# Start addresses of the matmul operands of a two-layer encoder, and the form of its weight list

## The chip, the core and the metric

The kernel runs on one core of one Trainium2 chip. The metric is the time of one execution on the device in microseconds; three executions of the kernel before are given below. The names of the engines are those of the profile: PE is TensorE (its matmuls; PEld are its weight loads), DVE is VectorE, ACT is ScalarE, POOL is GpSimd and SP is SyncE, whose queue SPq issues most transfers.

## The reference, cut to what matters

Two layers over 256 tokens of width 2048. Each layer is a token mixer and a gated MLP with a width-3 convolution over tokens; each is preceded by an RMS norm and added to the residual.

```python
for i in range(DEPTH):                       # DEPTH = 2, D = 2048, F = 5632
    h = rmsnorm(x, mix_norm_g[i])
    if i % 2 == 0:
        x = x + short_conv_mixer(h, ...)     # h @ (D, 3D), gates and conv, @ (D, D)
    else:
        x = x + dilated_attention_mixer(h, ...)  # h @ (D, 9D), 16 heads x 3 groups, @ (D, D)
    h = rmsnorm(x, ffn_norm_g[i])
    u = dwconv3(h @ w_up[i], ...)            # (D, 2F)
    a, b = split(u, 2)
    x = x + (silu(a) * b) @ w_down[i]        # (F, D)
return rmsnorm(x, final_norm_g)
```

Nearly all the arithmetic is in the products with the weight matrices, and each weight is read from device memory once and used once, for all 256 tokens.

## The kernel before

Activations are held transposed: a tile has 128 features on the partitions and the 256 tokens along the row. To keep more than the precision of the type float32r (four bytes an element), both operands of a product are split in a rounded part *hi* and a rest *lo*, so that a value is hi + lo. An activation row for one block k of 128 features holds 256 hi values and behind them 256 lo values, 512 in all (2048 bytes). Such tiles are `h` (input of the projections), `y` (input of the short convolution's output projection), `a` (input of the MLP's down projection, two buffers) and `o` (the attention's output). In `mm` these rows are the moving operand of TensorE, and a block of 128 x 128 weights is the stationary one, which PEld loads.

`load_w` fetches one column block of a weight matrix (1 MB, or 704 KB for the down projection) in a tile `raw` (four buffers) over the SP queue. `split` then makes, for up to 8 blocks at a time, the hi weights on ACT (line 72, a copy with rounding) and the lo weights on DVE (line 73, `raw - hi`), both into one tile `w2` (tag `w2`, four buffers): 8 hi blocks of 512 bytes, and behind them 8 lo blocks.

`mm` works through the tiles `w2` one after the other. For the blocks `now` that lie in the present tile it issues first the *hi matmuls*, each 512 columns wide (hi weights times the hi and lo halves of the row, line 102), then the *lo matmuls*, 256 columns wide (lo weights times the hi half, line 104). All add up in one tile `ps` in PSUM; `gathered` adds its two halves. The list that tells which blocks lie together is `parts`, pairs of a tile and a number, and the test is

```python
now = [k for k in ks if parts[k][0] is w2]
```

One hi matmul and its lo matmul are called a *pair* below. There are 5072 pairs with `h`, 1232 with `a`, 256 with `y` and 256 with `o`. Besides these:

- The first block of columns of the short convolution (lines 89 and 90, tile `w2s`) has 48 pairs in which hi and lo matmuls alternate, since there weights arrive block by block.
- The values of the attention (`v_unit`, lines 365 and 368, tile `w2v`, same buffers as `w2`) have the roles exchanged: `h` is stationary, the weights move. 768 pairs.
- The last quarter of the second layer's down projection (`last`, lines 242 to 244) issues, for each block, three matmuls of 256 columns in the order hi, lo, hi: 528 matmuls.

Pools are laid out in the row of a partition in the order in which they and their tiles are asked for: `const` (with `x`, `h` and small tiles), `weights` (`raw`, `w2`), `temps`, and behind them the pool of the running layer part (`y`, `a`, `o`, ...). Where the tiles begin follows from the sizes of all before them. The tile framework sets semaphores; each engine runs its instructions in the order of the program.

Of the kernel before, what the change touches and what calls it, by code (L numbers as in the profile page):

```python
# [10 lines left out]
F32 = mybir.dt.float32  # L11
F32R = mybir.dt.float32r
# [4 lines left out]
P = 128  # L17
T = 256
D = 2048
KT = D // P  # L20
FF = 5632
NF = FF // P
CH = 11
# [4 lines left out]
ALIBI_MAX = 8.0  # L28
SLOPES = [float(v) for v in (2.0 ** (-ALIBI_MAX * np.arange(1, H + 1) / H)).astype(np.float32)]
RAW = 4  # L30
QSCALE = float(P) ** -0.5


@with_exitstack
def encoder_kernel(ctx: ExitStack, tc: tile.TileContext, xT, gs, scw, fcw, dist, w_first, w_in, w_so, w_v, w_qk, w_ao, w_up, w_dn, out):
# [3 lines left out]
    pe, dve, act = nc.tensor, nc.vector, nc.scalar  # L39

    cp = ctx.enter_context(tc.tile_pool(name="const", bufs=1))
    wp = ctx.enter_context(tc.tile_pool(name="weights", bufs=1))
    tp = ctx.enter_context(tc.tile_pool(name="temps", bufs=2))
    pp = ctx.enter_context(tc.tile_pool(name="psum", bufs=4, space=bass.MemoryType.PSUM))

    x = cp.tile([P, KT, T], F32, name="x")
    h = cp.tile([P, KT, 2 * T], F32R, name="h")
    g_sb = cp.tile([P, 5, KT], F32, name="g_sb")
    scw_sb = cp.tile([P, KT, 4], F32, name="scw_sb")
    fcw_sb = cp.tile([P, 2, 2 * NF, 4], F32, name="fcw_sb")  # L50
    ones = cp.tile([P, P], F32, name="ones")
    ident = cp.tile([P, P], F32, name="ident")
    acc = cp.tile([P, T], F32, name="acc")
    rr = cp.tile([P, T], F32, name="rr")
    eps = cp.tile([P, 2], F32, name="eps")
    rc = cp.tile([P, 2], F32, name="rc")

    dve.memset(ones, 1.0)
    dve.memset(eps, EPS)
# [8 lines left out]
    def f32(ap):  # L68
        return ap.bitcast(F32)

    def split(hi, lo, src):
        ins = act.copy(hi, src)  # L72
        dve.tensor_sub(lo, src, f32(hi))  # L73
        return ins


    def load_w(src, n):
        raw = wp.tile([P, KT, P], F32, name="raw", tag="raw", bufs=RAW)
        nc.sync.dma_start(raw[:, :n, :], src)
        parts = []  # L80
        for k0 in range(0, n, 8):
            m = min(8, n - k0)
            w2 = wp.tile([P, 2, 8, P], F32R, name="w2", tag="w2", bufs=4)
            split(w2[:, 0, :m, :], w2[:, 1, :m, :], raw[:, k0 : k0 + m, :])
            parts += [(w2, k) for k in range(m)]
        return parts

    def mm1(ps, w, a, start, stop):
# [3 lines left out]
    def mm(ps, parts, a, ks):  # L92


        n = len(parts)
        ks = list(ks)
        while ks:
            w2 = parts[ks[0]][0]
            now = [k for k in ks if parts[k][0] is w2]
            ks = ks[len(now) :]  # L100
            for k in now:
                pe.matmul(ps, w2[:, 0, parts[k][1], :], a[:, k, :], start=k == 0, stop=False)  # L102
            for k in now:
                ins = pe.matmul(ps[:, :T], w2[:, 1, parts[k][1], :], a[:, k, :T], start=False, stop=k == n - 1)  # L104
        return ins

    def new_ps():
        return pp.tile([P, 2 * T], F32, name="ps", tag="ps", bufs=4)
# [31 lines left out]
    def squares(j):  # L140
        if j == 0:
            act.square(acc, x[:, j, :])
        else:
            sq = tp.tile([P, T], F32, name="sq", tag="sq")
            act.square(sq, x[:, j, :])
            dve.tensor_add(acc, acc, sq)
# [5 lines left out]
    def newton(r, v, t, whole=True):  # L152

        dve.tensor_mul(t, r, r)
        dve.tensor_mul(t, t, v)
        dve.tensor_scalar(t, t, -0.5, 1.5, op0=ALU.mult, op1=ALU.add)
        if whole:
            dve.tensor_mul(r, r, t)
# [78 lines left out]
    def last(ps, parts, a, j):  # L237

        xj = x[:, j, :]
        for k in range(CH):  # L240
            w2, i = parts[k]
            pe.matmul(ps[:, :T], w2[:, 0, i, :], a[:, k, T:], start=k == 0, stop=False)  # L242
            pe.matmul(ps[:, :T], w2[:, 1, i, :], a[:, k, :T], start=False, stop=False)  # L243
            pe.matmul(ps[:, :T], w2[:, 0, i, :], a[:, k, :T], start=False, stop=k == CH - 1)  # L244
        dve.tensor_add(xj, xj, ps[:, :T])
        if j < KT - 1:
            squares(j)
            act.mul(xj, xj, g_sb[:, 4, j : j + 1])
            return
        sq = tp.tile([P, T], F32, name="sq", tag="sq")  # L250
        act.square(sq, xj)
        st = pp.tile([P, 2 * T], F32, name="stat", tag="s", bufs=2)
        for n, src in enumerate((acc, sq)):
            for i in range(2):
                pe.matmul(
                    st[:, i : i + 1], src[:, i * P : (i + 1) * P], ones[:, 0:1], start=n == 0 and i == 0, stop=n == 1 and i == 1
                )
        dve.tensor_scalar_mul(xj, xj, g_sb[:, 4, j : j + 1])
        v = tp.tile([P, 2], F32, name="v", tag="m")
        dve.tensor_scalar(v, st[:, :2], 1.0 / D, EPS, op0=ALU.mult, op1=ALU.add)  # L260
        act.activation(rc, st[:, :2], AF.Sqrt, bias=eps[:, 0:1], scale=1.0 / D)
        dve.reciprocal(rc, rc)
        t = tp.tile([P, 2], F32, name="t", tag="den")
        newton(rc, v, t, False)

        dg = tp.tile([P, T], F32, name="dg", tag="e0")
        for i in range(2):
            dve.tensor_scalar(
                dg[:, i * P : (i + 1) * P], ident, rc[:, i : i + 1], t[:, i : i + 1], op0=ALU.mult, op1=ALU.mult
            )  # L270
        rb = pp.tile([P, 2 * T], F32, name="rb", tag="s", bufs=2)
        pe.matmul(rb[:, :T], ones, dg, start=True, stop=True)
        k0 = 0
        for n in (1, 2, 3, 4, 4, 2):
            ks = slice(k0, k0 + n)
            dve.tensor_mul(x[:, ks, :], x[:, ks, :], rb[:, :T].rearrange("p (a t) -> p a t", a=1).broadcast_to((P, n, T)))  # L276
            nc.sync.dma_start(out[:, ks, :], x[:, ks, :])
            k0 += n
# [50 lines left out]
    def attention():  # L329
        with tc.tile_pool(name="att", bufs=1) as sp:  # L330
# [9 lines left out]
            def norms():  # L340
                rms()
                dve.tensor_copy(rp.rearrange("p (i m) -> p i m", i=2), rr.rearrange("p (m i) -> p i m", i=2))
                dve.tensor_scalar_mul(rq, rp, QSCALE)
                for i in range(2):
                    ps = pp.tile([P, 2 * T], F32, name="stat", tag="s", bufs=2)
                    pe.transpose(ps[:, :P], rp[:, i * P : (i + 1) * P], ident)
                    dve.tensor_copy(rc[:, i : i + 1], ps[:, 0:1])

            def v_unit(hp, g):

                first = hp == 0 and g == 0
                if g == 0:
                    v = sp.tile([P, 2, 2, T], F32R, name="v", tag="v0", bufs=2)
                else:
                    v = sp.tile([P, 2, T], F32, name="v", tag=f"v{g}", bufs=2)
                ps = [new_ps(), new_ps()]
                for k0 in range(0, KT, 8):
                    raw = wp.tile([P, 8, T], F32, name="rawv", tag="raw", bufs=RAW)
                    nc.sync.dma_start(raw, w_v[3 * hp + g, :, k0 * T : (k0 + 8) * T])
                    for k1 in range(k0, k0 + 8, 4):  # L360
                        w2 = wp.tile([P, 4, 2, T], F32R, name="w2v", tag="w2", bufs=4)
                        split(w2[:, :, 0, :], w2[:, :, 1, :], raw[:, k1 - k0 : k1 - k0 + 4, :])
                        for k in range(k1, k1 + 4):
                            for i in range(2):
                                pe.matmul(ps[i], h[:, k, i * P : (i + 1) * P], w2[:, k - k1, :, :], start=k == 0, stop=False)  # L365
                        for k in range(k1, k1 + 4):
                            for i in range(2):
                                pe.matmul(  # L368
                                    ps[i][:, :T], h[:, k, T + i * P : T + (i + 1) * P], w2[:, k - k1, 0, :],
                                    start=False, stop=k == KT - 1,  # L370
                                )
                if first:
                    norms()
                for i in range(2):
                    tmp = tp.tile([P, T], F32, name="tmp", tag="tmp")
                    act.mul(tmp, ps[i][:, T:], rc[:, i : i + 1])
                    e = tp.tile([P, T], F32, name="e", tag="e0") if g == 0 else v[:, i, :]
                    dve.scalar_tensor_tensor(e, ps[i][:, :T], rc[:, i : i + 1], tmp, op0=ALU.mult, op1=ALU.add)
                    if g == 0:
                        split(v[:, i, 0, :], v[:, i, 1, :], e)  # L380
                vs[hp, g] = v
# [101 lines left out]
            for j in range(2):  # L483
                w = load_w(w_ao[j], KT)
                ps = new_ps()
# [5 lines left out]
            for j in range(KT):  # L491
                if j < 2:
                    ps, w = first[j]
                    mm(ps, w, o, range(KT - 1, KT))
                else:
                    w = load_w(w_ao[j], KT)
                    ps = new_ps()
# [90 lines left out]
```

## Time and profile before

| | |
|---|---|
| median of 3 executions | 2828.83 us (2828.40 to 2829.21) |
| the profiled execution | 2828.65 us, of which 2826.9 us from first to last instruction (span) |
| mean granted TensorE clock | 0.998 |
| PE busy / weight loads | 2810.6 us (99%) / 2465.7 us, 16388 each |
| DVE busy | 1995.9 us (71%) |
| ACT busy | 1505.3 us (53%) |
| bytes moved | 519.5 MB, 184 GB/s |

The page gives the time of a matmul from its start to a modelled end, and matmuls are pipelined: the next starts before the end of the last (a 512-column matmul is given 396 ns, but eight of them in a row start within less than 2 us). What a matmul costs is therefore read from start to start: in the timeline, where equal instructions that follow each other stand in one row with their first start, the difference of the starts of two rows divided by the count is the cost of one.

### The profile page before, as it was taken

What the parts mean: (1) busy time and instruction counts of PE and PEld (TensorE: products, weight loads), DVE (VectorE), ACT (ScalarE), POOL (GpSimd) and SP (SyncE); (2) the same over time, 40 slices, a digit from 0 to 9 for tenths busy, and PEclk for the clock granted to TensorE, in tenths of its full rate; (3) what the DMA queues carried; (4) which work ended last, traced back from release to release, by engine and by line L of the source; (5) the groups of instructions that cost most, each with busy time, mean ns of one, the idle gap of its engine ahead of it and who ended that gap; (6) DMA issues with size and microseconds to landing.
All of it is one profiled execution on the core that took longest, in us unless ns stands there. A gap on an engine that the chain in (4) does not pass through costs nothing.

```text
span 2826.9 us, 40841 instructions
## 1 busy us (share of the span) xinstructions
PE 2810.6 (99%) x16388; PEld 2465.7 (87%) x16388; DVE 1995.9 (71%) x3065; ACT 1505.3 (53%) x2320; POOL 0.7 (0%) x6
## 2 busy tenths in 40 slices
PE   9999999999999999999999999999999999999998
PEld 7888888888888888888888888888888888888888
DVE  7676787876867768665665666666778876777865
ACT  6444565555555546544444444444565555555555
POOL 0000000000000000000000000000000000000000
PEclk9999999999999999999999999999999999999999
DMA  7555555546555456544454454454455546546454
GB/s 254 199 181 192 191 183 192 182 166 214 184 166 210 168 186 218 182 175 170 174 178 168 175 179 167 176 179 168 175 190 184 193 161 211 188 164 214 169 181 143
DMA packets 79822, 519.50 MB, mean 184 GB/s; under 512 B 9104, under 2 KB 10256, under 8 KB 28816
## 3 DMA queue, kind: packets, MB, share of 16 engines
q1 hardware_dynamic: 79488, 516.37, 52.0%
q8 instruction: 128, 2.10, 0.3%
q14 instruction: 62, 0.51, 0.1%
q10 hardware_dynamic: 144, 0.52, 0.0%
HBM read 514.76 MB, written 2.10 MB: 183 GB/s over the span
## 4 chain that ended last, share of the span: by engine, by line
PE 99%; DMA 1%; DVE 0%; ACT 0%; SPq 0%; issue 0%; DVEq 0%; ACTq 0%
PE ps L102 56%; PE ps L104 28%; PE ps L365 6%; PE ps L368 3%; PE ps L242 1%; PE ps L244 1%; PE ps L243 1%; PE ot L456 1%; PE s L414 1%; PE pt L433 0%; PE ot L451 0%; DMA raw<-in_w_first 0%; DMA raw<-in_w_in 0%; DVE x L276 0%; PE s L400 0%; PE s L402 0%
## 5 line engine op out<-in xcount | busy, mean ns | idle before, releaser
L73 DVE TENSOR_TENSOR w<-raw,w 128x1024 fp32r<-128x1024 f32 (+1 forms) x954 | 1082.1, 1134 | 391.4 <-ACT w L72 372.5
L102 PE MATMUL ps<-h,w 128*128 128x512 f32 x5072 | 1289.6, 396 | 0.1
L72 ACT CAST w<-raw 128x1024 fp32r<-128x1024 f32 (+1 forms) x954 | 934.9, 980 | 553.5 <-PE ps L104 434.6
L102 PEld LDWEIGHTS ps<-h,w 128*128 128x128 f32 x5072 | 909.7, 188 | 169.0 <-ACT w L72 0.4
L104 PEld LDWEIGHTS ps<-h,w 128*128 128x128 f32 x5072 | 689.8, 188 | 58.2
L104 PE MATMUL ps<-h,w 128*128 128x256 f32 x5072 | 704.1, 281 | 0.0
L112 ACT COPY tmp<-ps 128x256 f32<-128x256 f32 x464 | 172.4, 372 | 500.4 <-PE ps L104 500.1
L114 DVE TENSOR_TENSOR e<-ps,tmp 128x256 f32<-128x256 f32 x464 | 196.2, 423 | 253.2 <-ACT tmp L112 253.2
L102 PE MATMUL ps<-a,w 128*128 128x512 f32 x1232 | 322.6, 394 | 0.0
L102 PEld LDWEIGHTS ps<-a,w 128*128 128x128 f32 x1232 | 215.4, 188 | 34.2
L365 PE MATMUL ps<-w2v,h 128*128 128x512 f32 x768 | 195.5, 396 | 0.0
L104 PEld LDWEIGHTS ps<-a,w 128*128 128x128 f32 x1232 | 175.8, 188 | 20.4
L73 DVE TENSOR_TENSOR w2v<-rawv,w2v 128x1024 fp32r<-128x1024 f32 x96 | 117.6, 1225 | 99.9 <-ACT w2v L72 98.5
L104 PE MATMUL ps<-a,w 128*128 128x256 f32 x1232 | 179.8, 279 | 0.0
L365 PEld LDWEIGHTS ps<-w2v,h 128*128 128x128 f32 x768 | 137.8, 188 | 25.3
L72 ACT CAST w2v<-rawv 128x1024 fp32r<-128x1024 f32 x96 | 100.7, 1049 | 97.6 <-PE ps L368 70.5
L368 PEld LDWEIGHTS ps<-w2v,h 128*128 128x128 f32 x768 | 104.6, 188 | 8.9
L126 ACT ACTIVATE cv<-e,fcw_sb 128x256 f32<-128x256 f32 x176 | 105.8, 602 | 12.1 <-DVE e L121 11.9
L368 PE MATMUL ps<-w2v,h 128*128 128x256 f32 x768 | 106.9, 281 | 0.0
L121 DVE TENSOR_TENSOR e<-e,rr 128x256 f32<-128x256 f32 x220 | 93.0, 424 | 6.8
L127 DVE SCALAR_TENSOR_TENSOR cv<-e,fcw_sb,cv 128x255 f32<-128x255 f32 x176 | 84.1, 479 | 8.0 <-ACT cv L126 8.0
L128 DVE SCALAR_TENSOR_TENSOR cv<-e,fcw_sb,cv 128x255 f32<-128x255 f32 x176 | 85.0, 484 | 6.1
(120 smaller groups left out, 1553.1 us busy)
## 6 DMA issues: line engine op xcount, KB each, us to landing
raw<-in_w_up SPq DMA_DIRECT2D x176, 1024.0 KB, 4.8
raw<-in_w_qk SPq DMA_DIRECT2D x96, 1024.0 KB, 4.8
raw<-in_w_dn SPq DMA_DIRECT2D x128, 704.0 KB, 4.0
rawv<-in_w_v SPq DMA_DIRECT2D x48, 1024.0 KB, 5.0
raw<-in_w_in SPq DMA_DIRECT2D x45, 1024.0 KB, 4.8
raw<-in_w_so SPq DMA_DIRECT2D x16, 1024.0 KB, 4.8
raw<-in_w_ao SPq DMA_DIRECT2D x16, 1024.0 KB, 4.7
raw<-in_w_first SPq DMA_DIRECT2D x3, 384.0 KB, 5.3
```

What stands on the lines that cost most here:

```text
L72: ins = act.copy(hi, src)
L73: dve.tensor_sub(lo, src, f32(hi))
L102: pe.matmul(ps, w2[:, 0, parts[k][1], :], a[:, k, :], start=k == 0, stop=False)
L104: ins = pe.matmul(ps[:, :T], w2[:, 1, parts[k][1], :], a[:, k, :T], start=False, stop=k == n - 1)
L112: act.copy(tmp, ps[:, T:])
L114: dve.tensor_add(e, ps[:, :T], tmp)
L121: dve.tensor_mul(e, g, r)
L126: act.activation(c, e, AF.Identity, bias=w[:, 3:4], scale=w[:, 1:2])
L127: dve.scalar_tensor_tensor(c[:, 1:], e[:, : T - 1], w[:, 0:1], c[:, 1:], op0=ALU.mult, op1=ALU.add)
L128: dve.scalar_tensor_tensor(c[:, : T - 1], e[:, 1:], w[:, 2:3], c[:, : T - 1], op0=ALU.mult, op1=ALU.add)
L365: pe.matmul(ps[i], h[:, k, i * P : (i + 1) * P], w2[:, k - k1, :, :], start=k == 0, stop=False)
L368: pe.matmul(ps[i][:, :T], h[:, k, T + i * P : T + (i + 1) * P], w2[:, k - k1, 0, :], start=False, stop=k == KT - 1,)
```

## The change

Four things are edited.

1. The small tiles `g_sb`, `eps` and `rc` are asked for ahead of `x` and `h`, and a tile of 64 bytes that nobody uses is added to the pool `temps`. Each tile `w2` grows from 8192 to 8448 bytes.
2. In a tile `w2` the lo weights begin 64 bytes later (`OFF`, 16 elements of four bytes).
3. In `v_unit` the moving weights begin 64 bytes behind the start of their tile.
4. An entry of `parts` now holds a pair of views `(hi, lo)` in place of the tile; `mm` and `last` take `hi` and `lo` from it.

This is where the operands begin in the two built programs, in bytes from a multiple of 256 (all steps between blocks are multiples of 512 bytes):

| operand | before | after |
|---|---|---|
| rows of `h` | 128 | 0 |
| rows of `y`, `a`, `o` | 192 | 0 |
| hi weights in `w2` | 0 | 0 |
| lo weights in `w2` | 0 | 64 |
| hi and lo weights in `w2s` | 192 | 0 |
| moving weights in `w2v` | 0 | 64 |

The fourth edit has an effect on the order. `load_w` writes `parts += [((hi, lo), k) for k in range(m)]`, which makes a new pair of Python objects for each k. The test `parts[k][0] is w2` in `mm` compares objects, so it now holds for one k alone: `now` has one block, and the loop issues one hi matmul and one lo matmul for each turn.

On PE, in the short convolution, where the first norm's sums (`stat`) stand between two weight tiles (numbers are buffer numbers; the second number of a size is the columns), before:

```order
L102 MATMUL ps<-h,w_506 128x512 x8
L104 MATMUL ps<-h,w_506 128x256 x8
L162 MATMUL stat<-acc,ones 128x256
L102 MATMUL ps<-h,w_509 128x512 x8
L104 MATMUL ps<-h,w_509 128x256 x8
```

and after:

```order
L108 MATMUL ps<-h,w_507 128x512
L110 MATMUL ps<-h,w_507 128x256
L170 MATMUL stat<-acc,ones 128x256
L108 MATMUL ps<-h,w_510 128x512
L110 MATMUL ps<-h,w_510 128x256
```

Eight hi matmuls and then eight lo matmuls have become hi, lo, hi, lo, eight times over (of each tile only the pair next to `stat` is shown after). All 6816 pairs of `mm` are moved in this way.

On PE, at the place where the first tile that `load_w` made (`w_278`, after `w_279`) is used, in between the last pairs of the first column block, before:

```order
L102 MATMUL ps<-h,w_278 128x512 x2
L89 MATMUL ps<-h,w2s 128x512 x3
L102 MATMUL ps<-h,w_278 128x512 x3
L90 MATMUL ps<-h,w2s 128x256 x3
L102 MATMUL ps<-h,w_278 128x512 x3
L104 MATMUL ps<-h,w_278 128x256 x8
```

and after:

```order
L108 MATMUL ps<-h,w_279 128x512
L94 MATMUL ps<-h,w2s 128x512 x3
L110 MATMUL ps<-h,w_279 128x256
L108 MATMUL ps<-h,w_279 128x512
L110 MATMUL ps<-h,w_279 128x256
L95 MATMUL ps<-h,w2s 128x256 x3
```

Here the first lo matmul of the tile stands second of its sixteen, and stood ninth before. The orders of POOL and SP are the same in both programs; ACT and DVE have a few rows exchanged at the end of the first column block and are otherwise the same.

```diff
+TPAD = 16
+OFF = 16
+W2 = 2 * 8 * P + 64
...
+    g_sb = cp.tile([P, 5, KT], F32, name="g_sb")
+    eps = cp.tile([P, 2], F32, name="eps")
+    rc = cp.tile([P, 2], F32, name="rc")
     x = cp.tile([P, KT, T], F32, name="x")
     h = cp.tile([P, KT, 2 * T], F32R, name="h")
...
-            w2 = wp.tile([P, 2, 8, P], F32R, name="w2", tag="w2", bufs=4)
-            split(w2[:, 0, :m, :], w2[:, 1, :m, :], raw[:, k0 : k0 + m, :])
-            parts += [(w2, k) for k in range(m)]
+            w2 = wp.tile([P, W2], F32R, name="w2", tag="w2", bufs=4)
+            hi, lo = (w2[:, z : z + 8 * P].rearrange("p (k c) -> p k c", k=8) for z in (0, 8 * P + OFF))
+            split(hi[:, :m, :], lo[:, :m, :], raw[:, k0 : k0 + m, :])
+            parts += [((hi, lo), k) for k in range(m)]
...
             w2 = parts[ks[0]][0]
             now = [k for k in ks if parts[k][0] is w2]
+            hi, lo = w2
             ks = ks[len(now) :]
             for k in now:
-                pe.matmul(ps, w2[:, 0, parts[k][1], :], a[:, k, :], start=k == 0, stop=False)
+                pe.matmul(ps, hi[:, parts[k][1], :], a[:, k, :], start=k == 0, stop=False)
             for k in now:
-                ins = pe.matmul(ps[:, :T], w2[:, 1, parts[k][1], :], a[:, k, :T], start=False, stop=k == n - 1)
+                ins = pe.matmul(ps[:, :T], lo[:, parts[k][1], :], a[:, k, :T], start=False, stop=k == n - 1)
+
+    tp.tile([P, TPAD], F32, name="padt", tag="padt", bufs=1)
...
-            w2, i = parts[k]
-            pe.matmul(ps[:, :T], w2[:, 0, i, :], a[:, k, T:], start=k == 0, stop=False)
-            pe.matmul(ps[:, :T], w2[:, 1, i, :], a[:, k, :T], start=False, stop=False)
-            pe.matmul(ps[:, :T], w2[:, 0, i, :], a[:, k, :T], start=False, stop=k == CH - 1)
+            (hi, lo), i = parts[k]
+            pe.matmul(ps[:, :T], hi[:, i, :], a[:, k, T:], start=k == 0, stop=False)
+            pe.matmul(ps[:, :T], lo[:, i, :], a[:, k, :T], start=False, stop=False)
+            pe.matmul(ps[:, :T], hi[:, i, :], a[:, k, :T], start=False, stop=k == CH - 1)
...
-                        w2 = wp.tile([P, 4, 2, T], F32R, name="w2v", tag="w2", bufs=4)
+                        w2 = wp.tile([P, W2], F32R, name="w2v", tag="w2", bufs=4)
+                        w2 = w2[:, OFF : OFF + 8 * T].rearrange("p (k z c) -> p k z c", k=4, z=2)
                         split(w2[:, :, 0, :], w2[:, :, 1, :], raw[:, k1 - k0 : k1 - k0 + 4, :])
```

More of the change, by code (lines that the diff above doesn't have):

```diff
@@ L44, in encoder_kernel @@
     pp = ctx.enter_context(tc.tile_pool(name="psum", bufs=4, space=bass.MemoryType.PSUM))
+    g_sb = cp.tile([P, 5, KT], F32, name="g_sb")
+    eps = cp.tile([P, 2], F32, name="eps")
+    rc = cp.tile([P, 2], F32, name="rc")
     x = cp.tile([P, KT, T], F32, name="x")
     h = cp.tile([P, KT, 2 * T], F32R, name="h")
-    g_sb = cp.tile([P, 5, KT], F32, name="g_sb")
     scw_sb = cp.tile([P, KT, 4], F32, name="scw_sb")
@@ L54, in encoder_kernel @@
     rr = cp.tile([P, T], F32, name="rr")
-    eps = cp.tile([P, 2], F32, name="eps")
-    rc = cp.tile([P, 2], F32, name="rc")
     dve.memset(ones, 1.0)
```

## The prediction

> **What bounds the kernel now.** I read the page's head first (is one engine the bound all along?), then the chain, then the waits of PE, and then starts in the timeline, because PE's busy time does not tell what a matmul costs.
>
> ```profile
> span 2826.9 us, 40841 instructions
> PE 2810.6 (99%) x16388; PEld 2465.7 (87%) x16388; DVE 1995.9 (71%) x3065; ACT 1505.3 (53%) x2320; POOL 0.7 (0%) x6
> PEclk9999999999999999999999999999999999999999
> PE 99%; DMA 1%; DVE 0%; ACT 0%; SPq 0%; issue 0%; DVEq 0%; ACTq 0%
> ```
>
> The chain that ended last is PE for 99% of the span, at a full clock throughout. So the time is a sum of costs of matmuls, and a change counts by what it does to the distance from one matmul's start to the next, or by a wait that it gives PE. PE hardly waits now:
>
> ```profile
> PE ps L89 <- ACT w2s L72: 4.8, 1, 4.8
> PEld ps L102 <- ACT w L72: 0.4, 1, 0.4
> ACT w L72 <- PE ps L104: 434.6, 347, 2.5
> ```
>
> The columns are total, number and longest. After the start, weights made PE wait once, for 0.4 us. The third row says who is ahead: 347 times ACT, which makes the hi weights, had to wait until PE's lo matmuls gave a buffer back.
>
> Now the cost of a pair (a hi matmul of 512 columns and its lo matmul of 256) by stage. Starts of groups of eight, with `y`, then with `h`:
>
> ```profile
> 299.72 2.02 PE L102 MATMUL ps<-y,w 128*128 128x512 f32 x8
> 301.58 1.07 PE L104 MATMUL ps<-y,w 128*128 128x256 f32 x8
> 302.50 2.02 PE L102 MATMUL ps<-y,w 128*128 128x512 f32 x8
> ...
> 391.96 2.03 PE L102 MATMUL ps<-h,w 128*128 128x512 f32 x8
> 393.83 1.12 PE L104 MATMUL ps<-h,w 128*128 128x256 f32 x8
> 394.78 0.39 PE L102 MATMUL ps<-h,w 128*128 128x512 f32 x1
> ```
>
> With `y`: hi (301.58 - 299.72)/8 = 232 ns, lo (302.50 - 301.58)/8 = 115 ns. With `h`: hi 234 ns, lo (394.78 - 393.83)/8 = 119 ns. The instructions are alike in shape, type and order; only the place of the operands differs. Whole stages (the last column of numbers is first and last start; `h` in the first layer's MLP, between 369 and 616.7 us):
>
> ```profile
> L102 PE MATMUL ps<-y,w x256: 388/396/398, 280.3 to 367.9; 128*128 128x512 f32 x128
> L104 PE MATMUL ps<-y,w x256: 276/276/281, 282.2 to 368.9; 128*128 128x256 f32 x128
> L102 PE MATMUL ps<-h,w x704: 390/393/581, 369.1 to 615.6; 128*128 128x512 f32 x176
> L104 PE MATMUL ps<-h,w x704: 274/281/287, 370.9 to 616.6; 128*128 128x256 f32 x176
> L242 PE MATMUL ps<-a,w x176: 276/276/276, 2753.3 to 2812.8; 128*128 128x256 f32 x176
> ```
>
> `y`: (369.1 - 280.3)/256 = 346.9 ns a pair. `h`: (616.6 + 0.1 - 369.1)/704 = 351.7 ns. So 4.8 ns a pair, 1.4%, hang on something that is no instruction. The last row is the cleanest: in `last`, every third of 528 matmuls of 256 columns stands in it, and each took (2812.8 - 2753.3)/525 = 113.3 ns, with one duration from minimum to maximum, though hi and lo alternate there. For `a` the down projection's 11 blocks give
>
> ```profile
> 620.58 2.02 PE L102 MATMUL ps<-a,w 128*128 128x512 f32 x8
> 624.43 1.79 PE L102 MATMUL ps<-a,w 128*128 128x512 f32 x7
> ```
>
> (624.43 - 620.58)/11 = 350 ns a pair. What the trace adds to the table of places: while a matmul streams its rows, the next weights are loaded, so what can collide is the running matmul's row and the next matmul's weights. In `y`, `a`, `o` these lie 64 bytes apart, counted round a multiple of 256 (192 and 0); in `h` they lie 128 apart. This is a reading, not shown: `a`, with the places of `y`, costs 3 ns more.
>
> **The change, part by part.** *Order.* The 6816 pairs of `mm` now alternate. One stage of the kernel alternates already, the first column block, where hi and lo follow each other in the stretch that is free of waits:
>
> ```profile
> 22.23 0.40 PE L89 MATMUL ps<-h,w2s 128*128 128x512 f32 x1
> 22.47 0.28 PE L90 MATMUL ps<-h,w2s 128*128 128x256 f32 x1
> 22.59 0.40 PE L89 MATMUL ps<-h,w2s 128*128 128x512 f32 x1
> ...
> 25.06 0.40 PE L89 MATMUL ps<-h,w2s 128*128 128x512 f32 x1
> ```
>
> Eight pairs from 22.23 to 25.06: 354 ns a pair, 0.24 us for hi and 0.12 for lo. Its row and weights lie 64 bytes apart too (128 and 192). It is slower than any grouped stage: the dear end of the price.
>
> *Places.* After the change the lo weights, loaded under a hi matmul, lie 64 from the row; the hi weights, loaded under a lo matmul, lie at the row's own distance, 0. For the first I take `y`'s hi, 232 ns, the nearest row in distance and width. For the second no row has distance 0 with such a neighbour; it lies between 113.3 (`last`) and 119 (`h`; the alternating stage's 0.12 us is no better), and I take the middle, 116. That makes 348 ns. The cheap end is the best that any row shows, 113 for 256 columns and twice that for 512: 339 ns. The dear end is 354, or, if distance 0 is bad in its own right, about `h`'s worst, 234 + 119 and some 4 ns more (as much as `h` has over `y`): 357.
>
> *The sum at 348.* `h`: 5072 x (348 - 351.7) = -18.8 us. `a`: 1232 x (348 - 350) = -2.5. `y`, and `o` taken as `y`: 512 x (348 - 346.9) = +0.6.
>
> *The values of the attention.* Row and weights stay grouped and go from 0 and 128 to 64 and 0:
>
> ```profile
> 1219.26 2.02 PE L365 MATMUL ps<-w2v,h 128*128 128x512 f32 x8
> 1222.06 1.33 PE L365 MATMUL ps<-w2v,h 128*128 128x512 f32 x5
> ```
>
> 350 ns a pair now (2.80/8). As 64 apart in `y` it would be 346.9, 768 x -3.1 = -2.4 us; but the 64 lie on the other side, and `h`'s price would be +1.3. I take 0.
>
> *`last`.* Two loads of three, those of hi weights under the second and third matmul of a block, come to lie at distance 0; the load of lo weights stays at 64. 352 matmuls by 0 to 5.7 ns (119 - 113.3) are 0 to +2.0 us; I take +0.5, since hi and lo alternate here at the floor already.
>
> *The wait for lo.* The first lo matmul of a tile now comes 0.23 us after its first hi matmul and came 1.85 us after; what is queued behind a waiting weight load is all of PE. Covered where DVE is a whole tile ahead, which four buffers and the row of ACT's waits (434.6 us) say of the steady part. The cover is thin only at the first tile:
>
> ```profile
> 25.61 1.23 DVE L73 TENSOR_TENSOR w<-raw,w 128x1024 fp32r<-128x1024 f32 x1 [2.07 <-ACT w L72]
> 25.63 0.73 PE L102 MATMUL ps<-h,w 128*128 128x512 f32 x2
> ```
>
> The lo weights are ready at 26.84, the first hi matmul starts at 25.63: PE could wait up to 1.0 us, less the three matmuls of the first block that stand in between (3 x 0.24). I take +0.4, and not more than 1.6 with a second such place.
>
> *Nothing else.* The unused tile and the moved small tiles issue nothing. SP's queue and POOL keep their orders; no DMA moves. ACT and DVE do the same shapes; were they a few per cent slower for their places, ACT's 434.6 us of waiting hides it.
>
> Sum: -18.8 - 2.5 + 0.6 + 0 + 0.5 + 0.4 = -19.8 us. The profiled execution took 2828.65 us, 1.75 more than its span and 0.2 under the median, so the forecast is 2809.
>
> [...]
>
> **The rivals.**
> 1. *The alternation costs what it costs in the first column block, and places don't help* (slower). For it: the only alternating rows of 512 and 256 are the dearest, 354, although 64 apart. Against: these 48 pairs run while data arrive, and `last` alternates at the floor. 5072 x 2.3 + 1232 x 4 + 512 x 7.1 = 11.7 + 4.9 + 3.6 = +20 us: 2849. The mean pair before is (5072 x 351.7 + 1232 x 350 + 512 x 346.9)/6816 = 351.0 ns; this rival decides from about 351.7 upwards, where 6816 x 0.7 and the +0.9 of the small terms make 5.7 us.
> 2. *All collisions go* (much faster). For it: 113.3 ns in `last` shows that 256 columns can be had at that price with hi and lo in turn. Against: no row shows 512 columns at 226. At 339: -64.4 - 13.6 - 4.0 = -82 us: 2747.
> 3. *No change.* Cost goes with neither place nor order but with the stage, or the two effects cancel (348 and 354 have 351 in their middle): 2829, within the 5.7 us (0.2%) that a measurement of this kernel can tell from no change. For it: `a` and `y` have the same places and differ by 3 ns. [...]
> 4. *PE comes to wait for DVE at every tile*: 1050 tiles by up to 1.6 us would add 1.7 ms. DVE's 71% and ACT's waits exclude it as a rule; a small chance is inside rival 1.
>
> **How the numbers follow.** Forecast (345 to 350 ns a pair, 2789 to 2823): 0.42. All collisions go, or most do (below 2789): 0.18. No change (2823 to 2834.5): 0.13. Slower: 0.27. The range leaves out the lower half of the second case and the upper part of the last (from 355.5 ns a pair, 6816 x 4.5 = +31 us): 2768 to 2860. The forecast's own range is 2789 to 2823. Faster 0.60, same 0.13, slower 0.27.
>
> **What would show it.** In the timeline after, `h`'s matmuls stand singly; hi 232 and lo 115 or 116 from start to start would show the step on places right, 236 and 118 rival 1, 226 and 113 rival 2. The stage of `h` in the first MLP should last 704 x 348 = 245 us (247.6 now). `last` should show a duration of 276 to 281 in place of 276 alone. PE's waits for DVE should stay under 2 us in total. What would make me wrong most likely is distance 0 under the lo matmul, for which no row stands, or the order's own price, for which only eight pairs do.

## The result and the profile after

The changed kernel takes 2802.68 us (median of 4 executions, 2801.87 to 2803.21), the kernel before 2828.8 us (median of 4 in the same comparison): a ratio of 0.9907 with a 95% interval of 0.989 to 0.9925. That is 26 us faster; 2809 was forecast. The profiled execution took 2801.87 us, its span is 26.8 us shorter.

From the page after, the span, the engines' busy times and the shares of the chain by engine:

```profile
span 2800.1 us, 40840 instructions
PE 2783.2 (99%) x16388; PEld 2470.5 (88%) x16388; DVE 1992.8 (71%) x3065; ACT 1504.0 (54%) x2320; POOL 0.7 (0%) x6
PE 99%; DVE 0%; DMA 0%; SPq 0%; ACT 0%; issue 0%; DVEq 0%; ACTq 0%
```

Of PE's waits for lo weights of the tiles `w2`, which the change could have added, the view of waits has one (in total, number, longest, in us):

```profile
PEld ps L110 <- DVE w L77: 0.4, 1, 0.4
```

The chain is still PE, with as many matmuls as before. The other waits of its weight loads grew by 0.4 us at the most from one profile to the other. So the matmuls cost less. The groups by tile, whole stages of `y` and of `h` in the first MLP (the same stretch as before, now from 365.6 us), and one of the three matmuls of `last`; after the colon stand minimum, median and maximum of the duration in ns, then first and last start in us:

```profile
L108 PE MATMUL ps<-y,w x256: 391/392/393, 277.0 to 365.4; 128*128 128x512 f32 x128
L108 PE MATMUL ps<-h,w x704: 391/392/587, 365.7 to 609.9; 128*128 128x512 f32 x176
L110 PE MATMUL ps<-h,w x704: 278/281/283, 366.0 to 610.1; 128*128 128x256 f32 x176
L250 PE MATMUL ps<-a,w x176: 278/281/283, 2724.8 to 2786.6; 128*128 128x256 f32 x176
```

`y`: (365.4 - 277.0)/255 = 346.7 ns a pair, unchanged. `h`: (610.1 + 0.1 - 365.7)/704 = 347.3, 351.7 before. The two stages are now alike. `last` is dearer: (2786.6 - 2724.8)/525 = 117.7 ns a matmul, 113.3 before. In the timeline, eleven pairs of `a` (first and last row) and a group of the attention's values:

```profile
615.08 0.39 PE L108 MATMUL ps<-a,w 128*128 128x512 f32 x1
615.31 0.28 PE L110 MATMUL ps<-a,w 128*128 128x256 f32 x1
...
618.89 0.39 PE L108 MATMUL ps<-a,w 128*128 128x512 f32 x1
```

```profile
1101.14 2.00 PE L374 MATMUL ps<-w2v,h 128*128 128x512 f32 x8
1102.99 1.10 PE L377 MATMUL ps<-w2v,h 128*128 128x256 f32 x8
1103.93 2.00 PE L374 MATMUL ps<-w2v,h 128*128 128x512 f32 x8
```

Eleven pairs of `a` take 3.81 us (618.89 - 615.08), 346 ns each, where they took 350; hi is 0.23 us. The values take (1103.93 - 1101.14)/8 = 349 ns.

Where the time went, as the sum of all distances from one matmul's start to the next in the two traces, by stage (`h`, `a`, `y` and `o` by the moving operand):

| matmuls | before, us | after, us | difference | forecast |
|---|---|---|---|---|
| `h`, 5072 pairs | 1787.5 | 1765.4 | -22.1 | -18.8 |
| `a`, 1232 pairs | 429.7 | 427.1 | -2.6 | -2.5 |
| `y` and `o`, 512 pairs | 178.2 | 178.3 | +0.1 | +0.6 |
| values, 768 pairs | 271.3 | 267.5 | -3.8 | 0 |
| `last`, 528 matmuls | 59.8 | 62.2 | +2.4 | +0.5 |

### The profile page after: what moved, and what is told of

It reads as the page before. It is cut to its first block, busy times and chain, and to the rows that moved or that the text cites. A ratio compares the mean times of both kernels' runs of the same rounds, so it can differ in the third digit from the quotient of the medians.

```text
span 2800.1 us, 40840 instructions
## 1 busy us (share of the span) xinstructions
PE 2783.2 (99%) x16388; PEld 2470.5 (88%) x16388; DVE 1992.8 (71%) x3065; ACT 1504.0 (54%) x2320; POOL 0.7 (0%) x6
## 4 chain that ended last, share of the span: by engine, by line
PE 99%; DVE 0%; DMA 0%; SPq 0%; ACT 0%; issue 0%; DVEq 0%; ACTq 0%
PE ps L108 56%; PE ps L110 29%; PE ps L374 6%; PE ps L377 3%; PE ps L251 1%; PE ps L250 1%; PE ps L252 1%; PE ot L465 1%; PE s L423 1%; PE pt L442 1%; PE ot L460 0%; PE ps L94 0%; DMA raw<-in_w_first 0%; PE ps L95 0%; DVE x L284 0%; PE s L411 0%
## 5 line engine op out<-in xcount | busy, mean ns | idle before, releaser
L108 PE MATMUL ps<-h,w 128*128 128x512 f32 x5072 | 1769.0, 393 | 0.0
L110 PE MATMUL ps<-h,w 128*128 128x256 f32 x5072 | 1417.8, 280 | 0.0
L108 PEld LDWEIGHTS ps<-h,w 128*128 128x128 f32 x5072 | 952.2, 188 | 201.4
L110 PEld LDWEIGHTS ps<-h,w 128*128 128x128 f32 x5072 | 962.8, 190 | 0.5 <-DVE w L77 0.4
L108 PE MATMUL ps<-a,w 128*128 128x512 f32 x1232 | 427.4, 392 | 0.0
L110 PE MATMUL ps<-a,w 128*128 128x256 f32 x1232 | 344.3, 280 | 0.0
L108 PEld LDWEIGHTS ps<-a,w 128*128 128x128 f32 x1232 | 231.2, 188 | 49.4
L110 PEld LDWEIGHTS ps<-a,w 128*128 128x128 f32 x1232 | 233.9, 190 | 0.0
```

The costliest lines, as they stand in the source:

```text
L108: pe.matmul(ps, hi[:, parts[k][1], :], a[:, k, :], start=k == 0, stop=False)
L110: ins = pe.matmul(ps[:, :T], lo[:, parts[k][1], :], a[:, k, :T], start=False, stop=k == n - 1)
```

## The experiments

The change does two things at once, places and order. Theory A: both count; a matmul and the weight load under it would disturb each other by the distance of their addresses, and the order says which distances meet. (That loads lie under matmuls is in the trace after: with `y`, the load for a lo matmul starts at 299.52 us, 0.01 us after the hi matmul ahead of it, and the lo matmul itself at 299.74.) Rival B: the order alone made the gain. Rival C: the places alone.

### Places without the order, and the order without the places

Places alone: the pair of views is made once for each tile, so that `now` holds eight blocks again.

```diff
-            parts += [((hi, lo), k) for k in range(m)]
+            pair = (hi, lo)
+            parts += [(pair, k) for k in range(m)]
```

> All start addresses of the changed kernel, but each tile's pair of views is made once, so that eight hi matmuls and then eight lo matmuls follow each other again, as before. Theory A (both count: the place sets how much a matmul and the next weight load disturb each other, and the order then decides which distances meet): the loads within a group lie at distance 0 under hi and under 256 columns at 64 minus 0, so h should land between the stage of y before (346.9 ns a pair) and h before (351.7): 2805 to 2825 us. Rival B (the order alone made the gain): h stays at 351 to 352 ns a pair, 2825 to 2832 us. Rival C (the places alone made it): 347 ns a pair, 2800 to 2805 us.

Measured: 2806.06 us, ratio 0.9921 (0.9906 to 0.9935) to before. Order alone, on the kernel before:

```diff
-            now = [k for k in ks if parts[k][0] is w2]
+            now = ks[:1]
```

> The kernel before with all its start addresses; only the list of blocks worked on in a turn is cut to one, so that hi and lo matmuls alternate. Theory A: row and next weights of h lie 128 bytes apart in both halves of a pair, as in no alternating stage so far; the first column block (64 apart, 354 ns) is the nearest, and a, y and o lose their 113 ns: 350 to 354 ns a pair, 2822 to 2850 us. Rival B (order alone): 347 ns a pair everywhere, 2800 to 2806 us. Rival C (places alone): unchanged within 4 us of 2829.

Measured: 2838.92 us, ratio 1.0037 (1.0022 to 1.0051). The stage of `y` in it:

```profile
L102 PE MATMUL ps<-y,w x256: 391/398/398, 282.1 to 372.2; 128*128 128x512 f32 x128
```

(372.2 - 282.1)/255 = 353.3 ns a pair, near the 354 of the first column block in the prediction. So rival B, that the order alone made the gain, falls: alternation at the old places costs 10 us. The places alone bring 22.6 us (2828.7 to 2806.06), nearly the whole gain, at the near end of what theory A gave. But rival C, the places alone, isn't the whole either. Order and places together are 3.4 us better than places alone (the intervals of the two ratios overlap, so the size is unsure), and order without places is 10 us worse, so the price of the order hangs on the places. These runs show that places and order both count; why they count, theory A's distances, they don't show.

### The 64 bytes

The offset of the lo weights (and of the moving weights in `v_unit`) is varied, with the changed kernel otherwise as it is. `OFF` counts elements of four bytes; it is 0 here and 8, 24, 32, 48 and 64 in the others.

```diff
-OFF = 16
+OFF = 0
```

> The changed kernel with the offset of lo weights (and of the moving weights in v_unit) at 0 in place of 64 bytes: everything begins at a multiple of 256. Theory A: the load of lo weights under a hi matmul goes from distance 64 to 0; hi goes from 230 ns to 232 to 236, lo stays at 117, together 2812 to 2845 us. Rival B (order alone): unchanged, 2802 within 3 us. Rival C (places of rows alone, the 64 bytes do nothing): also 2802 within 3 us.

> The changed kernel with the offset at 128 bytes in place of 64. Theory A: hi as with h before, 233 to 236 ns, lo at 117: 2820 to 2845 us. Rival B and rival C as for the offset 0: 2802 within 3 us.

> The changed kernel with the offset at 192 bytes in place of 64, so that lo weights lie a quarter of 256 bytes before a row's phase and not behind it. If only how far apart the two lie counts (64 either way): 2802 within 4 us. If the side counts too: between the offsets 0 (2817.9) and 128 (2819.6) or above, 2812 to 2830 us.

> The changed kernel with the offset at 32 bytes in place of 64. If accesses go by pieces of 64 bytes or more, 32 is the same as 0 (2818) or as 64 (2802) within 3 us. If the distance counts more finely, the time lies between the two, 2805 to 2815, or outside both.

> The changed kernel with the offset at 96 bytes in place of 64. By pieces of 64 bytes it is the same as 64 (2802) or as 128 (2820) within 3 us. If the distance counts more finely, between these, 2806 to 2816, or outside both (below 2798 would make it a better version).

> The changed kernel with the offset at 256 bytes in place of 64. If only the distance within 256 bytes counts, this is the run with the offset 0 again: 2818 within 3 us, hi of h 233.7 and lo 116.1 ns. If the period is longer (512 bytes or more), it lands elsewhere: 2800 to 2812 or above 2822 us.

| lo weights beyond a multiple of 256 | us | `y`, ns a pair | first MLP, ns a pair | second MLP, ns a pair |
|---|---|---|---|---|
| 0 | 2817.91 | 353 | 347 | 347 |
| 32 | 2806.68 | 347 | 347 | 347 |
| 64 (the change) | 2802.68 | 347 | 347 | 347 |
| 96 | 2814.10 | 352 | 347 | 347 |
| 128 | 2819.60 | 350 | 350 | 347 |
| 192 | 2821.18 | 347 | 350 | 350 |
| 256 | 2811.94 | 347 | 347 | 347 |

The last three columns are read from start to start: the stage of `y`, and in each layer's MLP the 352 pairs with `h` between its first and second turn of the down projection.

Each time but the change's is one execution. The spread is 18 us and 64 is the best of them, 15 us better than 0. By the ranges of the totals, 192 says that the side counts, 32 and 96 that the distance counts in steps finer than 64 bytes, and 256 that the period is longer than 256; 128 lies 0.4 us below its range. The stages don't bear these readings out. In both MLPs the offsets 0, 32, 64, 96 and 256 cost the same 347 ns. The offset 128 costs 350 in the first MLP and 347 in the second, with the same addresses and the same order; 192 costs 347 with `y`, as 64 does, and 350 in both MLPs. And 32 differs from 64 by 3.1 us in the values, while the sums of `h` and of `a` agree to 0.2 us. So what the totals compare is which stages run at 347 and which at 350 to 353, and the price of the values, whose weights the offset moves too; no rule for the offset is shown.

The offset 256 was to repeat the offset 0 and is 6 us faster. Where do they differ? Hi matmuls with `y` and `a`, first with the offset 0, then with 256:

```profile
L108 PE MATMUL ps<-a,w x1232: 390/392/396, 617.2 to 2739.3; 128*128 128x512 f32 x176
L108 PE MATMUL ps<-y,w x256: 394/398/404, 282.1 to 372.2; 128*128 128x512 f32 x128
```

```profile
L108 PE MATMUL ps<-a,w x1232: 391/391/395, 610.8 to 2733.0; 128*128 128x512 f32 x176
L108 PE MATMUL ps<-y,w x256: 392/394/395, 277.6 to 366.0; 128*128 128x512 f32 x128
```

From the first to the last row of `a` both take the same, 2122.1 and 2122.2 us. The whole difference arises before, among others in `y`: (372.2 - 282.1)/255 = 353.3 against (366.0 - 277.6)/255 = 346.7 ns. So three quarters of the kernel repeat at a step of 256 bytes, and the first part runs at another price, although its distances round 256 bytes and its order are the same.

### The same distances at other addresses

If only the distance of the row and the weights counts, `y` before (192 and 0) must cost the same at 0 and 64. Grouped again, with both weights 64 bytes beyond:

```diff
-            hi, lo = (w2[:, z : z + 8 * P].rearrange("p (k c) -> p k c", k=8) for z in (0, 8 * P + OFF))
+            hi, lo = (w2[:, z : z + 8 * P].rearrange("p (k c) -> p k c", k=8) for z in (OFF, 8 * P + OFF))
...
-            parts += [((hi, lo), k) for k in range(m)]
+            pair = (hi, lo)
+            parts += [(pair, k) for k in range(m)]
```

> The changed kernel, grouped again (eight hi, eight lo matmuls), with hi and lo weights both 64 bytes beyond a multiple of 256 and the rows at one. This gives every stage the distance and the order that y had before at other absolute addresses (192 and 0). Theory A' (only the distance round 256 bytes and the order count): 346.7 ns a pair everywhere, lo at 113 to 115 in h too, last at 113.3 ns a matmul: 2798 to 2806 us. Rival (the absolute address counts as well, a row must begin at 192 for 113 ns): lo at 117 to 120, 2810 to 2832 us.

Measured: 2803.63 us (one execution). The stage of `y`, and a group with `h`:

```profile
L109 PE MATMUL ps<-y,w x256: 388/396/398, 277.6 to 365.2; 128*128 128x512 f32 x128
L111 PE MATMUL ps<-y,w x256: 276/276/281, 279.5 to 366.2; 128*128 128x256 f32 x128
```

```profile
400.10 2.02 PE L109 MATMUL ps<-h,w 128*128 128x512 f32 x8
401.97 1.07 PE L111 MATMUL ps<-h,w 128*128 128x256 f32 x8
402.88 0.39 PE L109 MATMUL ps<-h,w 128*128 128x512 f32 x1
```

`y` has the durations that it had before, to the nanosecond, and the same length: 365.2 - 277.6 = 87.6 us from first to last hi matmul, as 367.9 - 280.3. `h`, which now has `y`'s distance, has `y`'s price: hi (401.97 - 400.10)/8 = 234, lo (402.88 - 401.97)/8 = 114 ns, where lo was 119 before (a start is given to 0.01 us, so a group of eight is good to about 1 ns). The rows of `a`, `y` and `o` have the same sums as before, to 0.1 us. So here an equal distance in an equal order had an equal price at other addresses. That it always has is not shown: the offsets 0 and 256 above differ with `y`. This version is as fast as the change, with hi dearer and lo cheaper.

The same places in alternation (the first line of the diff above without the second):

> The changed kernel in its own order (alternating), with the hi weights also 64 bytes beyond, so that row and next weights lie 64 apart under both matmuls. Theory A': the price of the first column block before and of y, a and o with the order alone, 235 + 118.3 = 353 ns: 2840 to 2850 us, dearer than the kernel before. Rival (64 apart is good by itself): 340 to 347 ns, 2755 to 2803 us.

Measured: 2845.28 us (one execution), 17 us over the kernel before:

```profile
L108 PE MATMUL ps<-y,w x256: 397/397/398, 281.5 to 371.6; 128*128 128x512 f32 x128
```

(371.6 - 281.5)/255 = 353.3 ns, the same as with the order alone, where `y` has this distance and order at other addresses. Hence 64 is not good by itself: of the places tried, the alternating order does best with hi weights at 0 and lo at 64. At the places of these two runs the alternation costs 42 us (2803.63 to 2845.28), at the old places 10, and at those of the change it costs nothing.

### Two attempts at a better version

The cheapest row was `last`: three matmuls of 256 columns at 113.3 ns are 340, less than a pair. So each pair becomes three, with the hi weights loaded twice and both weights 64 bytes beyond a multiple of 256, and `gathered` is no longer needed (which takes work from ACT and DVE: their busy times are 1353.1 and 1824.1 us there, 1504.0 and 1992.8 with the change). The loops over `now` become one; the other lines of the edit are left out here:

```diff
             for k in now:
-                pe.matmul(ps, hi[:, parts[k][1], :], a[:, k, :], start=k == 0, stop=False)
-            for k in now:
-                ins = pe.matmul(ps[:, :T], lo[:, parts[k][1], :], a[:, k, :T], start=False, stop=k == n - 1)
+                i = parts[k][1]
+                pe.matmul(ps[:, :T], hi[:, i, :], a[:, k, T:], start=k == 0, stop=False)
+                pe.matmul(ps[:, :T], lo[:, i, :], a[:, k, :T], start=False, stop=False)
+                ins = pe.matmul(ps[:, :T], hi[:, i, :], a[:, k, :T], start=False, stop=k == n - 1)
```

> A version that the rows point to. Each pair of 512 and 256 columns becomes three matmuls of 256 (hi weights with the lo half, lo weights with the hi half, hi weights again with the hi half), all added up in one half of the PSUM tile, as in last; so the hi weights are loaded twice and the two halves need no adding afterwards. Both weights 64 bytes beyond the rows. Theory A': 3 x 113.3 = 340 ns in place of 347, 6816 x -7 = -48 us against the changed kernel: 2745 to 2765 us. Rival (113 ns holds only at last's absolute addresses, otherwise 117 to 119): 3 x 118 = 354, 2840 to 2860 us.

Measured: 2827.64 us (10 executions, 2812.32 to 2829.93), ratio 0.9992 (0.998 to 1.0004). Neither expectation held. One of the three matmuls, in `y` and in `h`:

```profile
L109 PE MATMUL ps<-y,w x256: 276/276/276, 273.6 to 360.3; 128*128 128x256 f32 x128
L109 PE MATMUL ps<-h,w x649: 281/281/281, 370.8 to 599.7; 128*128 128x256 f32 x163
```

PE has 23204 matmuls in place of 16388. `y` runs at (360.3 - 273.6)/255 = 340.0 ns for three, as hoped, and every matmul alike. `h`, at the same distances in the same order, runs from 370.8 us on at (599.7 - 370.8)/648 = 353.2, also every one alike. The step between the two is not where `h` begins but where the norm's two matmuls (`stat`) come in, at 366.11 us:

```profile
364.06 0.28 PE L109 MATMUL ps<-h,w 128*128 128x256 f32 x1
...
366.11 0.59 PE L170 MATMUL stat<-acc,ones 128*128 128x256 f32 x2
...
366.89 0.28 PE L109 MATMUL ps<-h,w 128*128 128x256 f32 x1
...
370.77 0.28 PE L109 MATMUL ps<-h,w 128*128 128x256 f32 x1
```

The 18 matmuls with `h` ahead of `stat` take (366.11 - 364.06)/18 = 114 ns each, the 33 behind it (370.77 - 366.89)/33 = 118. So the same sequence settled at 113 in `y` and at 118 ns a matmul in `h` and kept that price for hundreds in a row, and here it changed where two other matmuls came between. `last` in the run with the order alone says the same: it has the addresses, the distances and the order of the kernel before, and yet

```profile
L242 PE MATMUL ps<-a,w x176: 280/282/282, 2762.5 to 2824.4; 128*128 128x256 f32 x176
```

is (2824.4 - 2762.5)/525 = 117.9 ns against 113.3. What comes ahead differs: there pairs alternate. The two runs with both weights 64 beyond say it once more: `last` is the same in both and takes 113.3 ns a matmul behind grouped pairs ((2788.4 - 2728.9)/525) and 117.7 behind alternating ones ((2829.9 - 2768.1)/525).

The second attempt joins two prices that looked independent, 113.3 ns for `y`'s lo matmuls (offset 192, alternating) and 230.9 for hi with `h` (grouped, offset 64): places alone with `OFF = 48`.

> Grouped again, rows and hi weights at multiples of 256, lo weights 192 bytes beyond one. With the offset 192 and alternation, y's lo matmuls took 113.3 ns; grouped with the offset 64 the hi matmuls took 230.9. If the two hold together: 230.9 + 113.3 to 115.5 = 344 to 346.5 ns a pair, 2782 to 2800 us, better than both kernels. Rival (which of its two prices, 113 or 118, a run of lo matmuls settles at is set by how the group begins, so the offset gives no hold on it): 117 to 119, 2803 to 2815 us.

Measured: 2815.83 us, ratio 0.9957 (0.9941 to 0.9974). The rival's price held, lo came to 118.0 ns on average in `h`; the time lies 0.8 us above its range. No version tried beats the change.

## Why the prediction was right, point by point

- **PE's spacing is the time, and it depends on where operands lie**: right, and shown by the run with the places alone, 22.6 us faster with the same instructions in the same order. Measured, the grouped lo matmuls of `h` cost 119 ns before and 114 with both weights 64 bytes beyond the rows, in the same order. No run shows whether it is the load that they lose this time to.
- **348 ns a pair with `h`**: measured 1765.4/5072 = 348.1. Of the two parts, hi was taken as 232 and is 230.9, lo as 116 and is 117.2; the errors cancel. The number was in part luck, since the reason given for it is not borne out: hi was priced by the lo weights' distance of 64, but in the MLPs the offsets 0, 32, 96 and 256 cost the same 347 ns a pair. What the pairs found there is a price that many places share. The gain came to 22.1 in place of 18.8 us mainly because the whole kernel's pair before is 1787.5/5072 = 352.4 ns, not the 351.7 of the first MLP.
- **`a`, `y`, `o`**: right in the sum. `a` gains on hi (286.4 to 282.9 us) and loses a little on lo (143.3 to 144.2 us).
- **Values**: mis-sized. 0 was taken, -3.8 us came. Of the terms for single stages it is the largest miss. Grouped as before, the values became cheaper when their distance went from 128 to 64 on the other side (hi 234.2 to 231.6, lo 119.0 to 116.6 ns).
- **`last`**: +0.5 was taken, +2.4 came, beyond the upper end of 2.0. The step that failed is "hi and lo alternate here at the floor already": the floor is one of two prices at which the sequence was seen to settle (113.3 and 117.7 ns). The miss is small against the total.
- **The wait for lo**: right, 0.4 us, once. That the matmuls stand while a weight load waits is seen in the same trace near its start, where loads and matmuls each have a longest wait of 4.8 us for the hi weights of `w2s`.
- **Rival 1** (alternation is dear) was right on the order by itself, 353 ns and +10 us; the places outweigh it. **Rival 2** did not come: no run shows 339 ns a pair. **Rival 3**, no change, falls by the result, and by the runs with one part each, which move the time by -22.6 and +10 us.

What stays open: what in the chip makes the places count, which of the shifted operands brought most of the 22.6 us, and what chooses among the prices at which a sequence settles. That the running matmul's row and the next weights' load disturb each other is the reading that the prediction started from. It fits the two runs with both weights 64 beyond, whose `y` costs what it cost at the same distance elsewhere (87.6 us from first to last hi matmul when grouped, 353.3 ns a pair when alternating); it does not explain the offsets, and no run here took the load away. Nor did a run move only the tiles of ACT and DVE, which the change moves too; that hundreds of matmuls in a row cost the same while those engines' work comes and goes speaks against them (the 649 of one row with `h` in the run with three of 256 all have 281 ns; DVE is busy for 65% of that run's span, ACT for 48%).

## What to carry to other kernels

Where PE is the bound, read the cost of a matmul from start to start by stage, and compare stages that issue the same instructions: a difference with no wait in it can lie in start addresses (here the places alone brought 22.6 us), and small shifts of a buffer are then worth a sweep (here 18 us between the best and the worst of seven offsets, six of them timed once). Read such a sweep by stage before making a rule of it. Judge order and places together: the same change of order cost 10 us at one set of places, 42 at another and nothing at a third. Compare built orders even when only views were meant to change: a test by object identity regrouped 6816 pairs.

## What the runs showed that I had not expected

The same sequence of matmuls at the same addresses ran at 113 or at 118 ns each (`last` before, 113.3, and with the order alone, 117.9), alike for hundreds in a row, and at a short interruption the price of a sequence changed (where two matmuls of the norm came between, from 114 to 118 ns in the run with three of 256). Pairs show it too, with 347 and 350 ns at the same offset of 128 in the two MLPs. With three matmuls in place of two, nine executions of ten took over 2827 us and one 2812, at the same granted clock (0.998; the nine had 0.997 to 0.999). A price that one stage shows is therefore not one that another stage with the same distances must have.
